# Split weights laid out in groups of four columns, with rings of their own for the two halves of the split

## The chip, the core and the metric

The kernel runs on one core of one Trainium2 chip. A core has a matrix engine (TensorE, PE in the profile, with its weight loads as PEld), a vector engine (VectorE, DVE), a scalar engine (ScalarE, ACT), GpSimd (POOL) and SyncE (SP), which here mainly issues DMA transfers. The on-chip memory SBUF has 128 partitions; TensorE reads its operands from SBUF and writes to PSUM, eight banks of 512 float32 per partition. The metric is the time of one execution on the device in microseconds; several runs are taken and their median is given.

## The reference

One layer of a decoder trunk in float32: 256 positions, model width 4096, 32 heads of 128. The convolution layer of the file is not reached (DEPTH is 1).

```python
h = x
h = h + attn_branch(rms_norm(h, norm_attn), w_in_attn, w_out_attn)
return rms_norm(h, final_norm)

def attn_branch(xn, w_in, w_out):
    q, k, v, g = split(xn @ w_in, 4)            # (256, 4096) @ (4096, 16384)
    o = stick_breaking_attention(q, k, v)       # per head, causal, in log space
    return (o * silu(g)) @ w_out                # (256, 4096) @ (4096, 4096)
```

The two projections are nearly all of the arithmetic. `stick_breaking_attention` needs, for each head, the scores z, a suffix sum over log(1 - sigmoid(z)), an exponential and a product with v.

## The kernel before

**Split operands.** [...] To keep float32 accuracy each operand is held as a high part (rounded by a copy into F32R) and a low part (the original minus the high part), and a product is three matmuls into one PSUM bank: high x high, high x low, low x high (`mm3`, lines 762 to 768). The stationary operand of such a matmul is a 128x128 block of activations, the moving operand 512 columns of weights.

**Units.** The weights' columns are cut into 20 units: 16 of the input projection (`units`, lines 268 to 271; each has the q, k, v and gate columns of two heads) and four of the output projection. A unit has 16 steps over the contraction, 256 rows each. At a step two weight tiles `raw` are loaded, [128, 2 blocks, 2 chunks of rows, 256 columns], from a ring of 7 (`load`, line 361). The first unit of each projection is "plain": 8 products a step. In the other units 10 of the 16 steps (`SEVEN`) get by with 7 products through sums of blocks, as in Strassen's method, and 6 take 8 products; in the last unit three more steps take 8. For the 7-product steps GpSimd issues a DMA that adds one chunk of rows to the other (`add_block`, line 380), and VectorE forms three more sums in place (`sums`, line 403).

**From raw weights to products.** `split` (line 442) walks the parts of the weights in the order of use. It takes a place in ring `w` (5 places, `PAIRS`: a high and a low tile [128, 2, 512] each) or, for parts of one chunk, in ring `s` (2 places), and starts `piece` (line 426): ScalarE copies `raw` to the high tile `wh` (a cast of 1024 or 512 elements per partition), VectorE subtracts (`minus`, line 264) and writes the low tile `wl`; then the raw tile may be given back (`low_done`). Both tiles hold their columns in one run: chunk c, then the two blocks of 256. `product` (line 1185) passes `wh[n][:, c, :]` and `wl[n][:, c, :]` to `mm3`. When a part's last product is through, `done` (line 1175) gives its place back.

**The order.** Nothing is decided on the chip. The class `Plan` (line 102) runs a small event simulation while the program is built: every piece of work has an engine, a cost, and a key (the time by which it is due, counted in products), and an engine takes the waiting work with the smallest key. `ring`, `take` and `give` are counters in that simulation which keep the number of live tiles of a tag under its number of buffers. The products themselves come in a fixed order (`products`, line 1197); TensorE's other work, that of the heads, goes between them.

**Beside the products.** When a unit's banks are full, `combine` (line 658) adds them into the tiles `one` and `two`; then the chain of its two heads (`heads`, `head`, `gated_with`, `gate`, lines 745 to 895) runs between the products of the next unit: transpose, scores, soft part on ScalarE and VectorE, suffix sum by a matmul with a triangle (`neg_tri`), exponential, product with v, gate. Its tiles have rings of one place each: `qkh`, `qkl`, `f`. The finished rows of two heads go out by DMA (`spill`) and come back as tile `p` for the output projection (`heads_of`, `blocks_of_heads`) through ring `gh`, which has three places. `gh` also serves the rows of x for the sums of squares (`x_stat`) and, at the end, the loads of x and of the final gain. The activations' stationary forms stay in SBUF all the time. During the output units the results `h` lie in a pool that takes the room of the attention's tiles (`make_room`, `new_h`), and the tail normalises and stores them.

Of the kernel before, what the change touches and what calls it, by code (L numbers as in the profile page):

```python
# [19 lines left out]
P = 128  # L20
S = 256
# [12 lines left out]

WARM, IDLE = 10, 640
# [8 lines left out]
PAIRS = 5  # L44
# [193 lines left out]
def kernel(  # L238
# [186 lines left out]

    def piece(n, c, there):

        p = parts[n]
        yield nc.until(*there)
        full = raw[p["tile"]][:, :, p["place"], :][:, :, c, :].rearrange("p i c n -> p c i n")  # L430
        h, l = (t[n][:, c, :].rearrange("p c (i n) -> p c i n", i=HG) for t in (wh, wl))
        size = (c.stop - c.start) * W
        key = first[n] - (AHEAD * 1e3 if p["seven"] and p["i"] < 2 else 0)
        yield act(lambda: nc.scalar.copy(h, full), size, key - 2.0 * 1e3)
        if n == 0:
            yield nc.until(("sh", c.start))
        yield dve(lambda: minus(l, full, h), size, key)
        for k in range(c.start, c.stop):
            nc.tell(("low", n, k))
        low_done(n)  # L440

    def split(size, tag, bufs):
        for n, p in enumerate(parts):
# [3 lines left out]
            yield nc.take(tag)  # L447
            t = p["tile"][1]
            yield nc.until(("raw", q, t))
            wh[n] = wp.tile([P, size, W], F32R, tag=tag + "h", name=f"wh{n}", bufs=bufs)  # L450
            wl[n] = wp.tile([P, size, W], F32R, tag=tag + "l", name=f"wl{n}", bufs=bufs)
# [8 lines left out]
    gcol = cp.tile([P, KC], F32, name="gcol")  # L460

# [47 lines left out]
    def blocks_of(i):  # L509

        key = place_of[0, i]
        tag = ("one", "two", "qkh", "qkl")[i % 4]
        yield nc.take(tag)
        y = ap.tile([P, KT, S], F32, tag=tag, name=f"xs{i}")
# [55 lines left out]
    for k in range(WARM):  # L570
        idle = wp.tile([P, IDLE], BF16, tag="gh", name=f"idle{k}", bufs=3)
        nc.vector.memset(idle, 0.0)
        nc.tensor.matmul(warm, idle[:, 0:P], idle[:, 0:W], start=True, stop=True)
# [11 lines left out]
    tri_f = ap.tile([P, P], F32, name="tri_f")  # L585
# [8 lines left out]
    def newton(r, v, name):  # L594

        e = cp.tile([P, 1], F32, name=f"{name}_e")
# [5 lines left out]
    ssq_x = cp.tile([P, NT, NQ], F32, name="ssq_x")  # L602
# [10 lines left out]
    def x_stat(i, t, q, w):  # L613
        xr = wp.tile([P, w], F32, tag="gh", name=f"xr{i}", bufs=3)
# [3 lines left out]
        yield nc.take("f")  # L618
        junk = ap.tile([P, w], F32, tag="f", name=f"junk{i}")
# [3 lines left out]
        nc.give("f", "gh")  # L623
        nc.tell(("stat", i))

    def x_factor():
        yield nc.until(*(("stat", i) for i in range(NT * NQ)))
        tot = cp.tile([P, NT], F32, name="ssq_xt")
# [6 lines left out]
        r = cp.tile([P, NT], F32, name="rin_r")  # L635
# [6 lines left out]
        rs["v"] = cp.tile([P, NT], F32, name="rin_v")  # L642
# [10 lines left out]
    def constants():  # L653
        yield nc.until(("used", 0, 1))
        yield dve(lambda: nc.vector.tensor_copy(neg_tri, tri_f), P)

# [88 lines left out]
    def gate(u):  # L745
# [3 lines left out]
        yield nc.take("qkl")  # L749
        l = ap.tile([P, NT, CW], F32, tag="qkl", name=f"gl{u}")  # L750
# [8 lines left out]
        nc.give("qkl")  # L759
# [17 lines left out]
    def head(u, i):  # L777
        yield nc.take("att", "qkh")
# [11 lines left out]
        qk = ap.tile([P, 2, S], F32, tag="qkh", name=f"qkT{u}_{i}")  # L790
# [11 lines left out]
        nc.give("qkh")  # L802
        yield nc.take("f")

        f = ap.tile([P, BW], F32, tag="f", name=f"f{u}_{i}")
# [17 lines left out]
        nc.give("f")  # L823
# [9 lines left out]
        nc.give("qkh", "qkl")  # L833
        yield nc.take("f")
        a = ap.tile([P, BW], F32, tag="f", name=f"a{u}_{i}")
# [20 lines left out]
        nc.give("f")  # L856
# [6 lines left out]
    def gated_with(u, i):  # L863
# [10 lines left out]
        if i == 0:  # L874
            yield nc.take("gh")
            st["o", u] = wp.tile([P, 4, P], F32, tag="gh", name=f"gated{u}", bufs=3)
# [20 lines left out]
    def heads_of(s, key, which=slice(0, 4)):  # L897

        yield nc.take("gh")
        y = wp.tile([P, 4, P], F32, tag="gh", name=f"p{s}", bufs=3)  # L900
# [39 lines left out]
    ssq_h = cp.tile([P, NT, NJ + 1], F32, name="ssq_h")  # L940
    mean_h = cp.tile([P, NT], F32, name="mean_h")
# [7 lines left out]
    def new_h(c):  # L949

        if c == NJ - 4:
# [4 lines left out]
        for t in range(NT):  # L956
            pool, tag, bufs = (ep, f"h{c}_{t}", 1)
            if c == NJ - 3 and t:
                pool, tag, bufs = wp, "gh", 3
# [13 lines left out]
    def load_out(c, t):  # L973
        pool, tag, bufs = (sp, "x" + "hl"[t] + str(LAST_STEPS[c - NJ + 4]), 1) if c >= NJ - 2 else (wp, "gh", 3)
# [6 lines left out]
    def load_gain(c):  # L981
        grow[c] = wp.tile([P, W], F32, tag="gh", name=f"grow{c}", bufs=3)
# [141 lines left out]
    def joined(t):  # L1124

        most[t] = cp.tile([P, 1], F32, name=f"most{t}")
# [4 lines left out]
    def finish(last, t, late):  # L1131
        v, r, f = (cp.tile([P, 1], F32, name=f"{n}{t}") for n in ("mean", "rout", "factor"))
# [42 lines left out]
    def done(n, k):  # L1175
# [4 lines left out]
        if count_down("part", n):  # L1180
            nc.give("w" if p["size"] == KT else "s")
# [3 lines left out]
    def product(n, k):  # L1185
# [6 lines left out]
            (wh[n][:, c, :], wl[n][:, c, :]),  # L1192
# [26 lines left out]
    together(split(KT, "w", PAIRS), split(1, "s", SINGLES), products(), x_stats(), x_factor(), constants())  # L1219
# [57 lines left out]
```

## Time and profile before

| | us |
|---|---|
| median of 3 runs (1739.35 to 1741.99) | 1740.06 |
| span of the profiled execution | 1738.8 |
| unit 0, from 8 to 94 us in the profile | 86.0 |
| one attention unit, 352.3 to 438.4 us | 86.1 |
| first output unit, 1385.9 to 1479 us | 93.1 |
| tail after the last matmul | 11.5 |

The profile is one execution of the program, taken by the hardware's profiler; the spans above are stretches of it. A row of the table by stretch gives the stretch, its length, then for each engine the time in which it was busy and how many instructions began, the granted TensorE clock as a share of the full one, the mean busy share of the DMA engines and the rate in GB/s. A row of a group of instructions gives line, engine, operation, output <- inputs, shapes and count, then the busy time in all, the mean length of one in ns, and the engine's idle time just before such instructions, with what ended it. Instructions of an engine overlap at their ends, so lengths are longer than the distance between two starts; for matmuls the ends are modelled, and only starts are used here. All instructions carry line 121, since one helper records them; they are told apart by their tiles: `acc` is a projection's PSUM bank, `sh`, `sl`, `oh`, `ol` are the stationary forms' parts, `z`, `tr`, `o` are the heads' banks.

### The profile page before, as it was taken

What the parts mean: (1) busy time and instruction counts of PE and PEld (TensorE: products, weight loads), DVE (VectorE), ACT (ScalarE), POOL (GpSimd) and SP (SyncE); (2) the same over time, 40 slices, a digit from 0 to 9 for tenths busy, and PEclk for the clock granted to TensorE, in tenths of its full rate; (3) what the DMA queues carried; (4) which work ended last, traced back from release to release, by engine and by line L of the source; (5) the groups of instructions that cost most, each with busy time, mean ns of one, the idle gap of its engine ahead of it and who ended that gap; (6) DMA issues with size and microseconds to landing.
All of it is one profiled execution on the core that took longest, in us unless ns stands there. A gap on an engine that the chain in (4) does not pass through costs nothing.

```text
span 1738.8 us, 24830 instructions
## 1 busy us (share of the span) xinstructions
PE 1722.9 (99%) x7735; PEld 1412.5 (81%) x7735; DVE 1643.5 (95%) x2106; ACT 1204.9 (69%) x1640; POOL 335.5 (19%) x407
## 2 busy tenths in 40 slices
PE   9999999999999999999999999999999999999997
PEld 6888888888888888888888888888888888878885
DVE  8889999999999999999999999999999987999997
ACT  7976767676767676767676767676767675666655
POOL 0022222222222221212222222222222112221220
PEclk9999999999999999999999999999999999999999
DMA  9967788878787878787878787878787878788895
GB/s 363 297 191 227 229 231 226 230 229 236 224 234 223 240 216 238 217 251 208 255 206 255 206 256 198 257 203 259 198 256 203 269 245 265 230 268 251 233 303 191
DMA packets 249380, 413.79 MB, mean 238 GB/s; under 512 B 28128, under 2 KB 73440, under 8 KB 249248
## 3 DMA queue, kind: packets, MB, share of 16 engines
q1 hardware_dynamic: 194544, 354.24, 60.6%
q0 software_dynamic: 54416, 57.70, 20.2%
q8 instruction: 60, 0.98, 0.2%
q14 instruction: 72, 0.59, 0.1%
q10 hardware_dynamic: 288, 0.28, 0.0%
HBM read 403.98 MB, written 8.13 MB: 237 GB/s over the span
## 4 chain that ended last, share of the span: by engine, by line
PE 78%; DVE 12%; issue 6%; ACT 2%; DMA 2%; SPq 0%; DVEq 0%; ACTq 0%
PE acc L121 74%; DVE wl L121 8%; DVE raw L121 3%; PE z L121 2%; PE o L121 1%; ACT wh L121 1%; DMA raw<-in_w_in_dram 1%; PE tr L121 1%; DVE gv_sb L121 1%; DVE h L121 0%; DMA raw<-in_w_out_dram 0%; DMA grow<-in_gain_out_dram 0%; DVE qk_sb L121 0%; SPq L121 0%; ACT sq L121 0%
## 5 line engine op out<-in xcount | busy, mean ns | idle before, releaser
L121 ACT CAST wh<-raw 128x1024 fp32r<-128x1024 f32 (+1 forms) x995 | 922.0, 971 | 406.1 <-issue 180.0
L121 DVE TENSOR_TENSOR wl<-raw,wh 128x1024 fp32r<-128x1024 f32 (+1 forms) x995 | 1068.8, 1123 | 58.4 <-ACT wh L121 56.6
L121 PE MATMUL acc<-wh,sh 128*128 128x512 f32 x1898 | 755.6, 398 | 0.0
L121 PE MATMUL acc<-wl,sh 128*128 128x512 f32 x1898 | 740.0, 390 | 0.8 <-DVE wl L121 0.8
L121 PE MATMUL acc<-wh,sl 128*128 128x512 f32 x1898 | 740.5, 390 | 0.0
L121 POOL DMA_DIRECT2D raw<-in_w_in_dram x300 | 262.9, 988 | 1078.9 <-DMA raw<-in_w_in_dram 427.4
L121 PEld LDWEIGHTS acc<-wh,sl 128*128 128x128 f32 x1898 | 356.3, 188 | 75.8 <-DVE sl L121 0.4
L121 PEld LDWEIGHTS acc<-wl,sh 128*128 128x128 f32 x1898 | 357.0, 188 | 73.8 <-DVE wl L121 2.8
L121 PEld LDWEIGHTS acc<-wh,sh 128*128 128x128 f32 x1898 | 356.8, 188 | 70.7 <-ACT wh L121 0.6
L121 DVE TENSOR_TENSOR raw<-raw,raw 128x512 f32<-128x512 f32 x354 | 243.4, 687 | 6.9 <-DMA raw<-in_w_out_dram 1.2
L121 PE MATMUL acc<-wl,oh 128*128 128x512 f32 x485 | 189.7, 391 | 2.0 <-DVE wl L121 1.8
L121 PE MATMUL acc<-wh,oh 128*128 128x512 f32 x485 | 190.0, 392 | 0.0
L121 PE MATMUL acc<-wh,ol 128*128 128x512 f32 x485 | 188.9, 389 | 0.0
L121 DVE TENSOR_TENSOR raw<-raw 128x512 f32<-128x512 f32 x177 | 121.0, 684 | 0.0
L121 PEld LDWEIGHTS acc<-wl,oh 128*128 128x128 f32 x485 | 91.1, 188 | 23.8 <-DVE wl L121 5.3
L121 PEld LDWEIGHTS acc<-wh,oh 128*128 128x128 f32 x485 | 91.0, 188 | 19.2 <-DVE gv_sb L121 0.5
L121 PEld LDWEIGHTS acc<-wh,ol 128*128 128x128 f32 x485 | 91.0, 188 | 18.8
L121 POOL DMA_DIRECT2D raw<-in_w_out_dram x54 | 47.1, 968 | 185.9 <-DVE wl L121 58.9
L121 ACT ACTIVATE f<-f 128x384 f32<-128x384 f32 x96 | 50.5, 526 | 3.0
L121 ACT COPY qkT<-tr 128x512 f32<-128x512 f32 x32 | 18.6, 581 | 24.1 <-PE tr L121 24.1
L121 ACT CAST oh<-p 128x512 fp32r<-128x512 f32 (+3 forms) x46 | 20.9, 467 | 18.8 <-DVE p L121 13.2
L121 DVE SCALAR_TENSOR_TENSOR gv_sb<-acc,rin_v,gv_sb 128x512 f32<-128x512 f32 x45 | 33.4, 741 | 0.0
(91 smaller groups left out, 750.3 us busy)
## 6 DMA issues: line engine op xcount, KB each, us to landing
raw<-in_w_in_dram SPq DMA_DIRECT2D x1024, 256.0 KB, 4.5
raw<-in_w_out_dram SPq DMA_DIRECT2D x256, 256.0 KB, 4.3
raw<-in_w_in_dram POOLq DMA_DIRECT2D x300, 128.0 KB, 4.7
p<-spill POOLq DMA_DIRECT2D x28, 256.0 KB, 4.2
raw<-in_w_out_dram POOLq DMA_DIRECT2D x54, 128.0 KB, 5.1
xr<-in_x_dram SPq DMA_DIRECT2D x16, 256.0 KB, 4.8
xres<-in_x_dram SPq DMA_DIRECT2D x16, 256.0 KB, 5.6
out_dram<-h SPq DMA_DIRECT2D x16, 256.0 KB, 2.8
```

The costliest lines, as they stand in the source:

```text
L121: return self.tc.keep_in_program_order(getattr(self.engine, name)(*args, **kw))
```

## The change

The diff does three things.

1. The high and low tiles of the weights are flat, [128, 1024], and are seen through `by_runs`: chunk c (2), block i (2) and groups of four columns are interleaved, so that a group of four neighbouring columns of one chunk and block lies in 16 bytes, and the next group of the same chunk and block starts sixteen elements further. The cast writes, the subtract reads and writes, and the matmul's moving operand reads with that pattern; `mm3` gives the PSUM side the same order of columns, so PSUM holds what it held. Parts of one chunk have both halves in one tile of ring `s`: the high part in the places of chunk 0, the low part in those of chunk 1.
2. Highs and lows have rings of their own: `w` with 7 highs, `wl` with 5 lows; the low place is taken after the cast has been given out.
3. Room is made for it. The heads' tiles `qkT`, `f`, `fh`, `fl`, `a` and the gate's `gl` go through ring `gh`, which has four places instead of three; two of the four tiles for x in unit 0 use ring `s`; the squares' scrap of `x_stat` goes to a PSUM bank; `tri_f` lies in a `gh` row until it is copied; small columns share one tile `scalars`; the sums of squares of x and of h share one tile; the results `h2` and `h3` lie in two high tiles and `h5` in two rows of `gh`.

```diff
+RUN = 4
-PAIRS = 5
+HIGHS = 7
+LOWS = 5
+ROWS = 4
...
-        ("raw", RAW_BUFS), ("w", PAIRS), ("s", SINGLES), ("gh", 3), ("one", 1), ("two", 1),
-        ("qkh", 1), ("qkl", 1), ("f", 1), ("att", 1), ("heads", 1),
+        ("raw", RAW_BUFS), ("w", HIGHS), ("wl", LOWS), ("s", SINGLES), ("gh", ROWS), ("one", 1), ("two", 1),
+        ("att", 1), ("heads", 1),
...
+    def by_runs(t):
+
+        return t.rearrange("p (h c i e) -> p c i h e", c=KT, i=HG, e=RUN)
+
     def piece(n, c, there):
...
-        full = raw[p["tile"]][:, :, p["place"], :][:, :, c, :].rearrange("p i c n -> p c i n")
-        h, l = (t[n][:, c, :].rearrange("p c (i n) -> p c i n", i=HG) for t in (wh, wl))
+        full = raw[p["tile"]][:, :, p["place"], :][:, :, c, :].rearrange("p i c (h e) -> p c i h e", e=RUN)
+        h = wh[n][:, c]
...
         yield act(lambda: nc.scalar.copy(h, full), size, key - 2.0 * 1e3)
+        if p["size"] == KT:
+            if c.start == 0:
+                yield nc.take("wl")
+                wl[n] = by_runs(wp.tile([P, KT * W], F32R, tag="wl", name=f"wl{n}", bufs=LOWS))
+                nc.tell(("lowslot", n))
+            else:
+                yield nc.until(("lowslot", n))
+        l = wl[n][:, c]
...
-            wh[n] = wp.tile([P, size, W], F32R, tag=tag + "h", name=f"wh{n}", bufs=bufs)
-            wl[n] = wp.tile([P, size, W], F32R, tag=tag + "l", name=f"wl{n}", bufs=bufs)
+            wh[n] = by_runs(wp.tile([P, KT * W], F32R, tag="wh" if size == KT else "s", name=f"wh{n}", bufs=bufs))
+            if size == 1:
+                wh[n], wl[n] = wh[n][:, 0:1], wh[n][:, 1:2]
...
+    scalars = cp.tile([P, 24], F32, name="scalars")
...
-        tag = ("one", "two", "qkh", "qkl")[i % 4]
+        tag = ("one", "two", "s", "s")[i % 4]
...
-        yield nc.take("f")
-        junk = ap.tile([P, w], F32, tag="f", name=f"junk{i}")
+        yield nc.take("att")
+        junk = att.tile([P, w], F32, tag="att", name=f"junk{i}")
...
     def mm3(out_, a, b, start, stop):
 
         (ah, al), (bh, bl) = a, b
+        if len(bh.shape) == 4:
+            out_ = out_.rearrange("p (i h e) -> p i h e", i=HG, e=RUN)
...
     def head(u, i):
-        yield nc.take("att", "qkh")
+        yield nc.take("att", "gh")
...
-        yield nc.take("f")
-
-        f = ap.tile([P, BW], F32, tag="f", name=f"f{u}_{i}")
+        yield nc.take("gh")
+
+        f = wp.tile([P, BW], F32, tag="gh", name=f"f{u}_{i}", bufs=ROWS)
...
-        yield nc.take("qkh", "qkl")
-        fh = ap.tile([P, BW], F32R, tag="qkh", name=f"fh{u}_{i}")
-        fl = ap.tile([P, BW], F32R, tag="qkl", name=f"fl{u}_{i}")
+        yield nc.take("gh", "gh")
+        fh, fl = (wp.tile([P, BW], F32R, tag="gh", name=f"f{k}{u}_{i}", bufs=ROWS) for k in "hl")
...
     def new_h(c):
 
+        if 2 <= c < NJ - 4:
+            pair = wp.tile([P, KT, W], F32, tag="wh", name=f"h{c}", bufs=HIGHS)
...
     def mixed_h(u, c):
         yield nc.until(("full", u, 1))
+        if c == 2:
+            yield nc.take("w", "w")
         if c == NJ - 4:
-            yield nc.take("raw", "gh")
+            yield nc.take("raw", "gh", "gh")
...
-            nc.give("w" if p["size"] == KT else "s")
+            nc.give(*(("w", "wl") if p["size"] == KT else ("s",)))
...
-            (wh[n][:, c, :], wl[n][:, c, :]),
+            (wh[n][:, c], wl[n][:, c]),
```

More of the change, by code (lines that the diff above doesn't have):

```diff
@@ L832, in head @@
         yield ten(scan, BW, BW, P, P)
-        nc.give("qkh", "qkl")
-        yield nc.take("f")
-        a = ap.tile([P, BW], F32, tag="f", name=f"a{u}_{i}")
+        nc.give("gh", "gh")
+        yield nc.take("gh")
+        a = wp.tile([P, BW], F32, tag="gh", name=f"a{u}_{i}", bufs=ROWS)
         def weights_of():
@@ L949, in new_h @@
     def new_h(c):
+        if 2 <= c < NJ - 4:
+            pair = wp.tile([P, KT, W], F32, tag="wh", name=f"h{c}", bufs=HIGHS)
+            for t in range(NT):
+                hs[c, t] = pair[:, t, :]
+            return
         if c == NJ - 4:
@@ L1131, in finish @@
     def finish(last, t, late):
-        v, r, f = (cp.tile([P, 1], F32, name=f"{n}{t}") for n in ("mean", "rout", "factor"))
+        v, r, f = (scalar_of_rows() for _ in range(3))
         second = ssq_h[:, t, NJ : NJ + 1]
```

68 lines of the change are left out of this document (40 added, 28 removed).

## The prediction

> **What bounds the kernel now.** I read the page's head first, then stretches of one projection unit each, then single matmuls.
>
> ```profile
> span 1738.8 us, 24830 instructions
> PE 1722.9 (99%) x7735; PEld 1412.5 (81%) x7735; DVE 1643.5 (95%) x2106; ACT 1204.9 (69%) x1640; POOL 335.5 (19%) x407
> PE 78%; DVE 12%; issue 6%; ACT 2%; DMA 2%; SPq 0%; DVEq 0%; ACTq 0%
> ```
>
> TensorE is busy for 99% of the span and holds 78% of the chain that ended last; VectorE stands just behind it with 95%. Busy shares alone do not say whether TensorE waits, so the next view is a table by stretch: unit 0, two attention units, the four output units, the tail.
>
> ```profile
> core 0: us, PE busy (x) PEld busy (x) DVE busy (x) ACT busy (x) POOL busy (x), PEclk, DMA share, GB/s
> 8.00:94.00 86.00, 85.23 (x373) 69.36 (x373) 74.45 (x132) 75.86 (x145) 3.85 (x5) 1.00 0.96 331
> 352.30:438.40 86.10, 86.10 (x392) 70.80 (x391) 82.95 (x102) 60.47 (x80) 18.40 (x23) 1.00 0.82 230
> 1299.80:1385.90 86.10, 85.92 (x391) 70.60 (x390) 82.84 (x102) 61.39 (x82) 18.06 (x22) 1.00 0.81 233
> 1385.90:1479.00 93.10, 93.06 (x423) 76.96 (x422) 77.76 (x133) 61.59 (x98) 15.48 (x26) 1.00 0.81 261
> 1479.00:1560.00 81.00, 79.88 (x350) 65.11 (x349) 78.25 (x97) 51.44 (x66) 15.63 (x18) 1.00 0.83 240
> 1560.00:1640.50 80.50, 79.57 (x348) 64.89 (x347) 80.15 (x96) 50.70 (x65) 18.56 (x22) 1.00 0.89 262
> 1640.50:1727.30 86.80, 86.77 (x381) 70.98 (x379) 82.34 (x115) 50.13 (x71) 11.01 (x13) 1.00 0.75 231
> 1727.30:1738.80 11.50, 0.00 (x0) 0.00 (x0) 4.21 (x12) 3.46 (x9) 0.00 (x0) 0.66 0.75 279
> ```
>
> In an attention unit (86.10 us) TensorE never stops, at the full granted clock (1.00). VectorE is busy 82.95 us of it, so 3.15 us remain there and 25.6 us on ScalarE. In the two middle output units VectorE already sets the pace: 80.15 of 80.50 us. So a unit can shorten in two ways only: a matmul takes less time, and VectorE then follows. What a matmul takes now comes from the chain in order of time (start, length, work) and from the timeline around one head:
>
> ```profile
> 307.05 0.81 PE o L121 x4
> 307.86 46.96 PE acc L121 x207
> 354.82 0.44 PE tr L121 x4
> ...
> 369.42 0.33 PE L121 MATMUL z<-fh,neg_tri 128*128 128x384 f32 x1
> 369.59 0.34 PE L121 MATMUL z<-fl,neg_tri 128*128 128x384 f32 x1
> 369.77 0.22 PE L121 MATMUL z<-fh,neg_tri 128*128 128x128 f32 x1
> ```
>
> 207 projection matmuls in 46.96 us are 226.9 ns each. Nothing but the stream of 512 columns fits in between: a 384-column matmul of the same kind starts its successor 0.17 us later (369.42 to 369.59), and 0.17/384 is 0.443 ns per column, as is 226.9/512. Time goes with the columns; there is no start cost to save. A mixed unit has 10 steps of 7 products and 6 of 8, 118 products of three matmuls, 354 x 0.2269 = 80.3 us; the remaining 5.8 us are its heads' own matmuls.
>
> **The change, part by part.** *Columns in groups of four.* The cast and the subtract write, and every projection matmul reads, runs of four elements (16 bytes) that lie sixteen elements apart. No instruction is added or removed. The rows it touches:
>
> ```profile
> L121 PE MATMUL acc<-wh,sh 128*128 128x512 f32 x1898 | 755.6, 398 | 0.0
> L121 PE MATMUL acc<-wh,oh 128*128 128x512 f32 x485 | 190.0, 392 | 0.0
> L121 ACT CAST wh<-raw 128x1024 fp32r<-128x1024 f32 x816 | 825.5, 1049 | 335.5 <-issue 138.8 <-PE acc L121 127.6 <-DVE raw L121 55.3
> ...
> L121 DVE TENSOR_TENSOR wl<-raw,wh 128x1024 fp32r<-128x1024 f32 x43 | 50.3, 1219 | 2.6 <-ACT wh L121 2.5
> L121 DVE TENSOR_TENSOR raw<-raw,raw 128x512 f32<-128x512 f32 x20 | 13.8, 688 | 0.3
> L121 DVE TENSOR_TENSOR wl<-raw,wh 128x512 fp32r<-128x512 f32 x10 | 6.8, 684 | 0.0
> ...
> 299.13 2.36 DVE L121 TENSOR_TENSOR wl<-raw,wh 128x1024 fp32r<-128x1024 f32 x2
> ```
>
> (The first three rows are counts of the whole run, the next three of the one unit 352.3 to 438.4, the last is from the timeline.) All 3 x (1898 + 485) = 7149 projection matmuls are concerned. No row shows a moving operand in short runs, so its price is bounded from both sides. Below, VectorE ends the gain: once a matmul is under (82.95 - 5.8)/354 = 217.9 ns, 9.0 ns less than now, the attention unit is VectorE's 82.95 us. Above, one lost column step for each group of four makes 226.9 x 5/4 = 283.6 ns. I take the lower end. The reason is that 0.443 ns per column is a rate, equal at 384 and 512 columns, so the feed of four-byte columns is what limits TensorE, and the order of addresses in that feed is the one thing of TensorE's work that the change alters. The rows give no sign, though; this is a choice and gets no more than its chance below. [...]
>
> For VectorE's and ScalarE's side I take nothing. The sums over raw (688 ns, two blocks of 256 with a hop) cost what the subtract in one run costs (684 ns); a hop after a long run is free, a hop after four elements no row shows. The subtracts of a unit are 50.3 + 6.8 = 57.1 us, so each per cent of stretch is 0.57 us on the engine that is to be the bound. The lower side could also be better: two subtracts in a row take 2.36 us, the second starting 1.14 us after the first, 0.08 less than its length, and the unit's 102 instructions packed in that way would fit in some 81 us. ScalarE's casts could take half as long again and still fit in its 25.6 us.
>
> *Separate rings.* Highs get seven places, lows keep five. Who waits today:
>
> ```profile
> ACT wh L121 <- PE acc L121: 150.0, 117, 3.5
> DVE wl L121 <- ACT wh L121: 56.6, 100, 1.7
> PE acc L121 <- DVE wl L121: 2.6, 5, 0.8
> ```
>
> ScalarE waits 150 us in all for a pair to come free from TensorE, VectorE 56.6 us for the cast, TensorE 2.6 us for the subtract. With TensorE as the bound, two more highs are worth at most those 2.6 us; with VectorE as the bound they let the casts run ahead and take away most of the 2.5 us per unit that VectorE idles before a subtract. That is what makes 82.95 us reachable and not 82.95 plus waits: no term of its own. The new wait for a low stands after the cast, with the same five lows as before, so nothing on ScalarE is queued behind it.
>
> *Heads' rows shared.* The heads' four private tiles go into the ring of four rows. By the chain above, head work ends at 307.86 and begins again at 354.82: 47 of 86.1 us are free, so the heads may run tens of us later before the next unit's results wait for their tiles: nothing. It bites where the last heads meet the loads of p, in the first output unit (1385.9 to 1479.0). I take 0.5 us there; its bounds are 0 and the heads' own 39 us (86.1 - 47) if they went wholly in series with the loads. The squares of x now go to a PSUM bank that no head uses in unit 0, the shared scalars serve a few small instructions at the end of unit 0 and in the tail: nothing, up to 1 us.
>
> **The sum**, against the profiled 1738.8 us: fifteen attention units, 15 x 3.15 = 47.2. Unit 0 has 384 matmuls, 384 x 9.0 ns = 3.5, but its DMA share is 0.96: I take 1.7. First output unit, 384 x 9.0 ns = 3.5 less 0.5: 3.0 (VectorE is at 77.76 of 93.10). Two middle output units: VectorE leaves 2.75 and 0.35, and most of that is waiting that it needs: 1.5 together. The last one: 363 x 9.0 ns = 3.3, VectorE leaves 4.46: 3.3. Tail of 11.5 us: 0. Together 56.7 us: 1682.1 us. The median of the runs is 1740.06, 1.3 us over the profiled time, so 1683.4 us.
>
> **The rivals.** *The groups cost TensorE nothing and bring nothing* (0.08). For it: runs as short as that might be one fetch like any other. TensorE then stays at 226.9 ns, everything else is hidden under it, and the time is 1738 to 1742 us. [...]
>
> *Each group costs TensorE a step* (0.14). If one step in seventeen is lost now and in future one for each group, a matmul takes 226.9 x 20/17 = 266.9 ns, and 7149 x 40 ns = 286 us: 2026 us; at 5/4 it is 2145 us. For it: the rate of 0.443 shows that something in this feed already has a limit; against it: nothing in the rows ties that limit to short runs. It decides from the first ns, since TensorE has no idle time.
>
> *VectorE's subtract stretches* (0.10). It reads one and writes one operand in groups. With TensorE unchanged it decides from 3.15/57.1 = 5.5% on; at 10% a unit is 2.6 us longer, twenty units some 50: 1790 us; at 25% 11.1 us a unit, 220 in all: 1960 us. Against it: every row of VectorE goes with the elements alone. [...]
>
> *The shared rows stall the first output unit* (0.04): forms of the heads come late and TensorE waits; with no gain elsewhere 5 to 20 us, 1745 to 1760 us. Against it: a loss that one unit can hold.
>
> **How the numbers follow.** My forecast has 0.64 with its own range of 1660 to 1720 us (VectorE packed to some 81 us per unit at the low end; a matmul that gains only a third of the 9 ns at the high end). Faster by over 0.2% (3.5 us, about what a measurement of this kernel can tell from no change) is that 0.64; within it 0.08; slower 0.14 + 0.10 + 0.04 = 0.28. To leave out no more than 2 in 10 the range must take in no change, the shared rows and the smaller stretches of VectorE, up to some 15%: 1660 to 1850 us. The step per group lies outside.
>
> **What would show it.** Right: in an attention stretch the chain gives 218 ns or less per projection matmul, VectorE is busy nearly without a gap, matmuls wait for wl, and the unit takes about 83 us. A matmul still at 227 ns is the first rival; 267 or more the second; a subtract of 128x1024 clearly over 1219 ns, the third; idle TensorE between 1386 and 1479 us of the old time, with casts of p late, the fourth. If the matmul is faster but the unit stays above 84 us, the forecast's step "VectorE can be packed" is wrong and not the one on the feed.

## The result, and the profile after

| | before | after |
|---|---|---|
| median of 9 runs each, us | 1740.23 (1739.06 to 1741.99) | 1736.38 (1734.59 to 1738.38) |
| ratio, 95% interval | | 0.9978 [0.9969, 0.9987] |
| span of the profiled execution, us | 1738.8 | 1734.4 |

The change saves 3.9 us; the forecast was 57. The time lies between the 1660 and 1850 us that the prediction gave in all, since these took in no change, and outside the 1660 to 1720 us of the forecast itself. (One of the six runs of *narrow*, further below, took 7647.81 us and is left out of its median.) The head of the profile page after, and its table by stretch (columns as before; all instructions now carry line 124):

```profile
span 1734.4 us, 25312 instructions
PE 1709.5 (99%) x7735; PEld 1413.1 (81%) x7735; DVE 1634.4 (94%) x2106; ACT 1209.9 (70%) x1640; POOL 334.7 (19%) x407
```

```profile
core 0: us, PE busy (x) PEld busy (x) DVE busy (x) ACT busy (x) POOL busy (x), PEclk, DMA share, GB/s
180.00:266.00 86.00, 84.93 (x389) 70.45 (x388) 82.64 (x103) 60.68 (x79) 17.23 (x21) 1.00 0.82 231
352.00:438.00 86.00, 85.62 (x392) 70.86 (x392) 81.86 (x101) 60.84 (x79) 18.25 (x22) 1.00 0.82 228
1386.00:1479.00 93.00, 93.00 (x428) 77.65 (x427) 76.42 (x132) 59.52 (x96) 14.90 (x25) 1.00 0.79 242
1637.00:1722.90 85.90, 85.55 (x378) 70.19 (x376) 81.72 (x115) 50.02 (x71) 10.99 (x13) 1.00 0.74 233
```

The work is what it was: 7735 matmuls, 2106 instructions on VectorE. The attention units are still about 86 us long, the clock is still 1.00, but TensorE, which was busy for 86.10 of 86.10 us, now stands for 1.1 and 0.4 us in the two shown. In the first output unit it does not stand at all.

For the length of units one instruction serves as a marker: ScalarE's `qk_sb<-gv_sb`, which runs once per attention unit. The view of that tile, before and after (count, shortest, median and longest in ns, then the first and the last start):

```profile
L121 ACT ACTIVATE qk_sb<-gv_sb,rin_v x15: 724/725/727, 178.8 to 1384.3; 128x512 f32<-128x512 f32 x15
```

```profile
L124 ACT ACTIVATE qk_sb<-gv_sb,scalars x15: 719/724/728, 180.2 to 1383.6; 128x512 f32<-128x512 f32 x15
```

Between the first and the last lie 14 units: 1205.5 us before (86.11 each), 1203.4 after (85.96 each). So of the 4.4 us between the two profiles, the start up to the first marker loses 1.4, the attention units gain 2.1 and the rest, output units and tail, 3.7 (1738.8 - 1384.3 = 354.5 against 350.8). This division of the span into three is used for every kernel below.

What one matmul takes is read from the chain in order of time (start, length, what), in the attention and the output units of the changed kernel:

```profile
1333.17 45.73 PE acc L124 x203
...
1455.04 82.93 PE acc L124 x368
```

45.73/203 and 82.93/368 are both 225.3 ns, where it was 226.9. The groups have saved 1.6 ns of a matmul, not 9.0. Times 7149 that is 11.4 us, and even of this only a third is seen. The row groups of one unit and of the whole run show that the other engines' instructions did not change in length:

```profile
L124 DVE TENSOR_TENSOR wl<-raw,wh 128x1024 fp32r<-128x1024 f32 x42 | 50.2, 1218 | 3.2 <-ACT wh L124 1.8 <-PE acc L124 1.3
L124 ACT CAST wh<-raw 128x1024 fp32r<-128x1024 f32 x816 | 826.0, 1046 | 294.5 <-DVE raw L124 183.0 <-PE acc L124 88.5 <-issue 11.9
```

The subtract takes 1218 ns (1219 before), the cast 1046 (1049). The table of waits (who waits for whom: us in all, times, longest) has new rows:

```profile
DVE wl L124 <- PE acc L124: 31.3, 46, 2.1
DVE wl L124 <- ACT wh L124: 30.9, 53, 0.9
PEld acc L124 <- DVE qk_sb L124: 13.6, 14, 1.5
PE acc L124 <- DVE qk_sb L124: 7.6, 14, 1.1
```

VectorE's waits for casts have fallen from 56.6 to 30.9 us, as the two more highs were meant to do (whether it is they is taken up under *pairs_again*), but 31.3 us of a new wait have come: VectorE stands with a subtract in hand until TensorE gives a low place back. And in 14 units TensorE now waits for `qk_sb`, a sum that `combine` does on VectorE when a unit's banks are full. No such row was there before. The timeline at one of these places (start, length, work, and in brackets the idle time before it and who ended it):

```profile
351.59 0.74 DVE L124 SCALAR_TENSOR_TENSOR qk_sb<-acc,scalars,qk_sb 128x512 f32<-128x512 f32 x1
352.25 0.68 DVE L124 TENSOR_TENSOR raw<-raw,raw 128x512 f32<-128x512 f32 x1
352.85 0.68 DVE L124 TENSOR_TENSOR wh<-raw,wh 128x512 fp32r<-128x512 f32 x1
353.45 0.68 DVE L124 TENSOR_TENSOR raw<-raw,raw 128x512 f32<-128x512 f32 x1
354.06 1.22 DVE L124 TENSOR_TENSOR wl<-raw,wh 128x1024 fp32r<-128x1024 f32 x1
355.19 0.74 DVE L124 SCALAR_TENSOR_TENSOR qk_sb<-acc,scalars,qk_sb 128x512 f32<-128x512 f32 x1
355.99 0.50 PE L124 MATMUL acc<-wh,sh 128*128 128x512 f32 x1 [0.38 <-DVE qk_sb L124]
```

VectorE works without a gap here, in its order; the second sum comes at 355.19 because other work stands before it in that order, and the bank that it frees comes too late for the matmul. VectorE's 3 us of idle time per unit did not keep it from being late.

### The profile page after: what moved, and what is told of

It reads as the page before. It is cut to its first block, busy times and chain, and to the rows that moved or that the text cites. A ratio compares the mean times of both kernels' runs of the same rounds, so it can differ in the third digit from the quotient of the medians.

```text
span 1734.4 us, 25312 instructions
## 1 busy us (share of the span) xinstructions
PE 1709.5 (99%) x7735; PEld 1413.1 (81%) x7735; DVE 1634.4 (94%) x2106; ACT 1209.9 (70%) x1640; POOL 334.7 (19%) x407
## 5 line engine op out<-in xcount | busy, mean ns | idle before, releaser
L124 DVE TENSOR_TENSOR wl<-raw,wh 128x1024 fp32r<-128x1024 f32 (+1 forms) x818 | 974.6, 1217 | 67.5 <-PE acc L124 31.3
L124 PE MATMUL acc<-wh,sh 128*128 128x512 f32 x2048 | 784.8, 395 | 8.1 <-DVE qk_sb L124 7.6
L124 PE MATMUL acc<-wh,sl 128*128 128x512 f32 x1898 | 732.8, 386 | 0.5 <-DVE sl L124 0.5
L124 PE MATMUL acc<-wl,sh 128*128 128x512 f32 x1748 | 675.7, 387 | 1.5 <-DVE wl L124 1.5
L124 PEld LDWEIGHTS acc<-wh,sh 128*128 128x128 f32 x2048 | 384.6, 188 | 92.4 <-DVE qk_sb L124 13.6
L124 PEld LDWEIGHTS acc<-wl,sh 128*128 128x128 f32 x1748 | 328.3, 188 | 63.9 <-DVE wl L124 4.4
L124 PE MATMUL acc<-wl,oh 128*128 128x512 f32 x458 | 177.3, 387 | 1.9 <-DVE wl L124 1.9
L124 DVE TENSOR_TENSOR wh<-raw,wh 128x512 fp32r<-128x512 f32 x177 | 120.8, 683 | 2.0 <-ACT wh L124 2.0
L124 PEld LDWEIGHTS acc<-wh,oh 128*128 128x128 f32 x512 | 96.0, 188 | 19.1
L124 PEld LDWEIGHTS acc<-wl,oh 128*128 128x128 f32 x458 | 85.8, 187 | 21.1 <-DVE wl L124 4.4
```

The source lines that it names most:

```text
L124: return self.tc.keep_in_program_order(getattr(self.engine, name)(*args, **kw))
```

## The experiments

First the change is taken apart, then a matmul's time, then a unit's; last comes the plan's price. The three columns of spans are the division above, in us, from each kernel's profiled execution; the last two columns are its runs. The kernel before, run beside them, had medians of 1739.9 us (layout_only to layout_paced), 1740.4 (sweeps_before to narrow_sums) and 1740.3 (the last two).

| kernel | first marker | one unit | rest | median of n, us | ratio, 95% interval |
|---|---|---|---|---|---|
| before | 178.8 | 86.11 | 354.5 | | |
| after | 180.2 | 85.96 | 350.8 | 1736.38 of 9 | 0.9978 [0.9969, 0.9987] |
| layout_only | 178.2 | 85.98 | 352.8 | 1736.71 of 11 | 0.9982 [0.9974, 0.9991] |
| rings_only | 179.5 | 86.33 | 352.9 | 1740.48 of 11 | 1.0004 [0.9995, 1.0013] |
| pairs_again | 177.8 | 85.63 | 360.0 | 1737.51 of 11 | 0.9985 [0.9976, 0.9994] |
| narrow | 176.2 | 85.99 | 352.2 | 1734.71 of 5 | 0.9972 [0.9960, 0.9984] |
| after_paced | 178.0 | 85.76 | 351.5 | 1732.68 of 5 | 0.9959 [0.9945, 0.9973] |
| layout_paced | 178.3 | 86.41 | 352.3 | 1743.12 of 11 | 1.0019 [1.0010, 1.0028] |
| sweeps_before | 177.8 | 86.39 | 355.9 | 1744.55 of 10 | 1.0025 [1.0015, 1.0034] |
| sweeps_rings | 180.4 | 86.34 | 355.5 | 1746.22 of 6 | 1.0038 [1.0025, 1.0051] |
| sweeps_paced | 181.5 | 86.50 | 369.1 | 1761.23 of 4 | 1.0118 [1.0103, 1.0133] |
| narrow_sums | 176.1 | 86.47 | 354.3 | 1741.64 of 10 | 1.0010 [1.0001, 1.0020] |
| narrow_low | 175.0 | 83.79 | 344.5 | 1695.53 of 4 | 0.9743 [0.9728, 0.9758] |
| narrow_rings | 178.7 | 85.51 | 349.0 | 1728.44 of 4 | 0.9934 [0.9917, 0.9950] |

Each division is of one execution. The runs of one kernel spread over 1.5 to 9 us, and the profiled execution of rings_only is the longest of its 11 (1742.71 us, 2.2 above their median), so tenths of a microsecond between two kernels' units are not certain.

### The change taken apart

*layout_only*: the kernel before with the groups of four alone (`by_runs`, flat tiles, the places of parts of one chunk); rings and heads' rows as before.

```diff
+    def by_runs(t):
+        return t.rearrange("p (h c i e) -> p c i h e", c=KT, i=HG, e=RUN)
```

> The kernel before with the groups of four alone, rings and heads' tiles as before. Theory A (the groups make each projection matmul shorter, from a start-to-start mean of 227.3 ns to 225.5 ns, and the new rings give part of it back): 7149 x 1.8 = 12.7 us less, 1727 to 1731 us, and no new wait of TensorE at the start of a unit. Theory B (the groups bring nothing, the rings the small gain): 1740 us, 227 ns per matmul.

*rings_only*: the changed kernel with its columns in one run again.

```diff
-        return t.rearrange("p (h c i e) -> p c i h e", c=KT, i=HG, e=RUN)
+        return t.rearrange("p (c i h e) -> p c i h e", c=KT, i=HG, e=RUN)
```

> The changed kernel with the weights' columns in one run per chunk and block again (chunk, block, column), everything else as changed. Theory A: the matmuls are back at 227.3 ns and the waits of the new rings stay, 1743 to 1750 us. Theory B: 1736 us.

The groups alone give 0.9982, all of the change's gain within the intervals; the rings and the shared rows alone give 1.0004, nothing that can be told from no change. The table says why the two do not add up to more: in the output units both gain (1.7 and 1.6 us, together 3.3, the change has 3.7), but in the attention units the rings lose 0.22 us a unit (86.33, in that longest execution) where the groups gain 0.13. Of the two expectations the one that gives the gain to the groups is nearer, but layout_only was to fall to 1731 us or less and rings_only to rise to 1743 or more; neither did. The same waits for `qk_sb` that the changed kernel has (7.6 us of TensorE's matmuls, 13.6 of its weight loads) are in the rings' kernel (3.9 and 10.2); with the old rings no matmul of a projection waits for it, and its weight loads do so only in layout_paced, 4.2 us in 14 places of at most 0.3.

One more thing goes with the rings, which the description of the change leaves out: a part of one chunk now takes its place in ring `s` after its raw tile has landed, not before (`split`). It is in rings_only, pairs_again and narrow_rings, and not in layout_only.

*pairs_again*: the changed kernel, but the low place is taken together with the high one, before the cast, instead of between cast and subtract.

```diff
-        if p["size"] == KT:
-            if c.start == 0:
-                yield nc.take("wl")
...
-                yield nc.take(tag)
+                yield nc.take(tag, "wl")
```

> The changed kernel, but the place for the low part is taken together with that for the high part, before the cast is given out, so that ScalarE and not VectorE waits for it. If VectorE's wait for a low place (31 us in 46 waits, new with the change) is what makes the sums at a unit's end late (TensorE waits 0.4 to 1.3 us per unit for them): those waits go, 1728 to 1732 us. If the late sums have another cause (the order of VectorE's work, the shared rows): 1735 to 1738 us.

Its waits:

```profile
ACT wh L124 <- PE acc L124: 204.3, 93, 3.7
DVE wl L124 <- ACT wh L124: 32.2, 73, 0.7
DVE wl L124 <- PE acc L124: 3.5, 5, 1.5
```

VectorE's wait for a low place falls from 31.3 to 3.5 us. ScalarE, which has room, now waits 204.3 us for TensorE instead of 133.1, though before the casts of single chunks and not of pairs (139.0 and 65.3 us; 44.6 and 88.5 in the changed kernel). The waits for `qk_sb` are gone, and the attention units take 85.63 us, 0.33 less than in the changed kernel. So the place of that wait, with the order that the plan wrote around it, is what made the sums late: a wait on VectorE stands before everything queued behind it, sums of banks among it. The time does not show it, because 9.2 us more go in the rest of the run, and about half of that at one place in the first output unit:

```profile
1447.82 0.75 PE L124 MATMUL acc<-wh,oh 128*128 128x512 f32 x1 [3.15 <-ACT oh L124]
1448.36 0.63 PE L124 MATMUL acc<-wl,oh 128*128 128x512 f32 x1
1448.79 0.63 PE L124 MATMUL acc<-wh,ol 128*128 128x512 f32 x1
```

A cast of activations (`oh`) is late, TensorE stands for 3.15 us, and for some 3 us after that its matmuls start every 430 ns. The granted clock from 1447.8 to 1451.8 us is 0.57 (0.91 over the 20 us from 1440 to 1460). The stall is a matter of the plan's order, which came out differently.

The run also bears on the two more highs. A high and a low are taken together and given back together here, so the plan never has more than five pairs out, as before the change. Still VectorE's waits for casts are 32.2 us, about what they are in the changed kernel (30.9), and in the three units from 344 to 602 us they are these, first in layout_only, then here:

```profile
DVE wl L122 <- ACT wh L122: 7.6, 15, 0.6
DVE wl L124 <- ACT wh L124: 5.2, 12, 0.6
```

Both kernels have the groups and at most five pairs; the first has units of 85.98 us, the second of 85.63. They differ by the heads' shared rows, the smaller changes that made room, the later place in ring `s`, and the plan's order. So it is not shown that two more highs shortened the waits for casts; the shared rows are a rival that no run tries by itself.

### What a matmul's time is made of

*micro_one*: a kernel that only multiplies, 24 cases of 30 matmuls in a row, operands at rest in SBUF; the reference's computation is left out. The cases change the moving operand's pattern or the stationary one's.

```diff
+        ("run", lambda k: mov[:, 0:512], seq),
+        ("onecolumn", lambda k: mov[:, 0:1].broadcast_to([P, 512]), seq),
+        ("oneweight", lambda k: mov[:, 0:512], lambda k: st[:, 0:1].broadcast_to([P, P])),
+        ("grpa", lambda k: groups(4, 16, 0), seq),
+        ("aftera", lambda k: after(0), seq),
...
+        ("half", lambda k: mov[:, 0:256], seq),
+        ("bf", lambda k: mb, lambda k: sbf[:, 128 * (k % 8) : 128 * (k % 8) + 128]),
```

> Leaves the whole computation out; 30 matmuls of 512 columns in a row per case, other engines idle, start-to-start times read. Theory C (the moving operand alone pays, one step per 64 bytes read): one run 227 ns, a moving operand of one column repeated 214 to 216 ns, a stationary operand of one column repeated still 227 ns, groups of four sixteen apart either 216 or 267 ns in all four positions alike. [...]

The chain in order of time; a case's length by 30 is its matmul, and the clock is 1.00 throughout:

```profile
29.24 6.80 PE run L178 x30
36.04 6.56 PE onecolumn L178 x30
42.60 6.88 PE oneweight L178 x30
49.48 6.87 PE grpa L178 x30
...
63.49 7.39 PE grpc L178 x30
...
78.01 6.67 PE aftera L178 x30
...
112.88 14.44 PE runtwo L178 x30
...
177.02 3.60 PE half L178 x30
180.62 3.30 PE quarter L178 x30
183.92 6.50 PE bf L178 x30
```

`run` is the kernel before: 226.7 ns. `half`, 256 columns, takes 120.0. The difference for 256 columns is 106.7 ns, 0.4167 ns each, and what is left over is 13.3 ns per matmul. Two sizes always give such a split; that the plan's price, 0.4167 x n + 13.4, has the same two numbers speaks for it. At 128 columns it does not hold: `quarter` takes 110.0 ns, not 66.7. Two-byte operands (`bf`) take 216.7 ns by the chain, 3.4 above 512 x 0.4167 = 213.3. What the 13 ns are is looked for in the cases that change one operand: one column repeated as moving operand takes 218.7 ns, so feeding the same word over and over takes away eight of them; one column repeated as stationary operand (`oneweight`, 229.3) takes away none; groups of four, sixteen apart, take 229.0 or 246.3 by where in the sixteen they begin (`grpa`, `grpc`); the changed kernel's own pattern 222.3 for one chunk and 227 for the other; and stationary blocks in steps of 2 to 16 words 233 to 235. Both operands' patterns matter, the stationary block's (226.7 against 233 to 235 ns) in a way that no run explains. The theory of the expectation does not hold: by it, groups of four were to take the same time at every place in the sixteen, where 229.0 and 246.3 ns came, and one column repeated as moving operand 214 to 216, where 218.7 came. The step per 64 bytes from which it starts was the author's supposition; no run shows it. What the 13 ns are stays open.

Runs of two words, sixteen apart (`runtwo`), take 481 ns, twice the time. So these groups of 8 bytes are far worse, and groups of four are not free by themselves: at `grpc` they cost 20 ns (246.3 against 226.7).

*micro_two*: the same with the kernel's own sequence, 28 products of three matmuls on seven highs and five lows, in 16 patterns; again the matmuls alone.

```diff
+        ("asbefore", plain, straight),
+        ("asafter", inter("h c i e"), straight),
...
+        ("ordsixteen", order(16, 4), placed(16, 4)),
...
+        ("longeight", order(4, 8), placed(4, 8)),
```

> Leaves the whole computation out; 28 products of three matmuls per case with the kernel's operand sizes (seven high and five low tiles, seven stationary blocks per step), other engines idle. With the columns in one run 227 ns; as in the change 222 to 227 ns. [...]

The tile view of four of them (the first of a product's three matmuls; shortest, median and longest in ns, first and last start):

```profile
L169 PE MATMUL asbefore<-wh,sh x28: 389/389/389, 30.9 to 49.3; 128*128 128x512 f32 x28
L169 PE MATMUL asafter<-wh,sh x28: 382/384/398, 50.0 to 68.2; 128*128 128x512 f32 x28
L169 PE MATMUL ordsixteen<-wh,sh x28: 434/438/448, 186.6 to 208.9; 128*128 128x512 f32 x28
L169 PE MATMUL longeight<-wh,sh x28: 380/381/399, 295.2 to 313.1; 128*128 128x512 f32 x28
```

Tenths of a microsecond are too coarse here; read to the hundredth from the timeline, from a case's first start to the last of its 84, a matmul takes 226.7, 225.6, 276.0 and 220.2 ns. The pattern of the change is worth 1.1 ns of the 13 with no other engine at work, somewhat less than the 1.6 in the kernel. Other orders of reading cost up to 50 ns, and one, four sweeps of eight words, wins 6.5. Both times of the expectation came: 226.7 ns where 227 was expected, 225.6 where 222 to 227 was.

*sweeps_before, sweeps_rings, sweeps_paced*: that order in the whole kernel; columns stay in one run, only the matmul reads (and PSUM is written) in four sweeps; in the kernel before, with the new rings, and with the plan's price of a matmul at 220 ns.

```diff
+        out_, bh, bl = (t.rearrange("p (h b e) -> p b h e", b=4, e=8) for t in (out_, bh, bl))
```

> The kernel before; only the projection matmuls read their 512 columns in another order, four sweeps over runs of eight columns that lie 32 apart, and write PSUM in that order (matmuls alone: 220.0 ns on the mean, against 226.7). If VectorE and its waits for casts set 86.0 us per attention unit, as with the shortened matmuls: 86.0 us per unit and 1733 to 1738 us, no better than 8.9 ns less per matmul. If TensorE were still the bound: 354 x 6.7 ns = 2.4 us less per unit, 1690 to 1700 us.

> The same reading order on the changed kernel's rings, with the columns stored in one run. It shows what pace VectorE keeps with seven highs, five lows and four shared rows. If the rings free VectorE from its waits (82 to 83 us busy per unit): 84 us per unit, 1700 to 1712 us. If they only move the waits (to low places and to the sums at a unit's end): 85.5 to 86 us, 1728 to 1736 us.

> The same with the planner's price of a 512-column matmul at 220 ns instead of 226.7. If the written order is what costs TensorE its waits: 5 to 15 us less than the same kernel with the old price; if VectorE's own chain is the bound: within 5 us of it.

All three are slower than before, by 0.25, 0.38 and 1.18%, and all three outside what was expected. Inside sweeps_before a matmul starts on average 228.4 ns after the one before it (mean of all distances up to 250 ns; 227.3 by the same count in the kernel before), not 220. The chain shows that this mean is a mixture:

```profile
184.45 11.90 PE acc L121 x54
...
220.77 47.78 PE acc L121 x207
...
270.97 12.46 PE acc L121 x54
```

In one unit 54 matmuls take 220.4 ns each, as they do alone; the 54 at the same place of the next unit take 230.7, and the 207 between them 230.8. The other work is alike in the two stretches of 54 (VectorE busy for 95% of both, DMA share 0.71 and 0.69), which speaks against a plain contest for the memory. What chooses between the two times is open; no run separates it.

### What holds a unit at 86 us

*narrow*: the kernel before with the second and third matmul of each product on 480 of the 512 columns (the low parts' products of the last 32 columns are left out). It makes TensorE faster without a pattern: by the same count of distances a matmul takes 220.4 ns on the mean instead of 227.3, 7 ns less where 8.9 were expected.

```diff
+        out_, bh, bl = out_[:, 0:NARROW], bh[:, 0:NARROW], bl[:, 0:NARROW]
         nc.tensor.matmul(out_, ah, bl, start=False, stop=False, **kw)
```

> The kernel before; the second and third matmul of each product take 480 of their 512 columns, the rest of the low parts' contribution is left out. That shortens a projection matmul by 32 x 2/3 x 0.4167 = 8.9 ns on the mean, the 9.0 ns of the forecast, and changes nothing else. If VectorE can be packed as the forecast had it: 83 us per attention unit and 1680 to 1690 us in all. If the written order and VectorE's queue hold it back (TensorE then waits for the sums at a unit's end and for the heads): 84 to 85.5 us per unit, 1700 to 1725 us.

A unit still takes 85.99 us, longer than either expectation, though TensorE alone needs only 83.8 (narrow_low, below). TensorE's waits for `wl` have risen from 2.6 to 17.3 us in the run. Two views of narrow, the table by stretch, and VectorE's waits in three units:

```profile
430.00:516.00 86.00, 84.81 (x392) 70.54 (x391) 82.94 (x102) 60.69 (x81) 18.04 (x21) 1.00 0.80 231
```

```profile
DVE wl L122 <- ACT wh L122: 7.6, 15, 0.6
DVE f L122 <- ACT f L122: 0.5, 3, 0.2
```

VectorE: 82.94 us busy, 2.5 us per unit in waits for casts of at most 0.6 us, 0.2 us for the heads; 85.6 in sum. It was as long as a unit already before the change, 0.1 us behind TensorE's 86.1.

*narrow_sums*: the same, with the sums of blocks planned 7 us ahead of their product instead of 3 (`SUMS_AHEAD`), to give VectorE other work while a cast runs.

```diff
-AHEAD, SUMS_AHEAD = 4.0, 3.0
+AHEAD, SUMS_AHEAD = 4.0, 7.0
```

> The kernel before with 480 of 512 columns in the second and third matmul of each product, and the planner's lead for the sums over raw raised from 3 to 7 us, so that a sum stands earlier in VectorE's order and its cast is done when VectorE comes to the subtract. If the waits of VectorE for these casts (2.5 us per unit) hold it at 86.0 us: those waits shrink and the unit falls to 83.5 to 85 us, 1690 to 1715 us. If the pace of 86.0 us has another cause: 86.0 us and 1735 us as before.

The units became longer (86.47), and the waits for casts rose from 51.2 to 58.8 us over the run. A miss: this knob does not fill the gaps.

*narrow_low*: narrow (on 240 of each 256 columns), and VectorE's subtract on 240 of 256 columns as well; the low parts of one column in sixteen are left out.

```diff
-        yield dve(lambda: minus(l, full, h), size, key)
+        yield dve(lambda: minus(l[:, :, :, 0:SHORT], full[:, :, :, 0:SHORT], h[:, :, :, 0:SHORT]), size, key)
```

> The kernel before, with the second and third matmul of each product on 2 x 240 of the 512 columns, as in the narrow run, and VectorE's subtract on 240 of the 256 columns of each block (1024 elements become 960). TensorE's floor per attention unit falls to about 83 us as in narrow; VectorE's work falls by 57.1 x 1/16 = 3.6 us, some 3.2 us counted by starts. If VectorE's own work plus its waits set the 86.0 us in narrow: units of 83 to 83.5 us, 1685 to 1697 us in all. If something else holds the unit (ScalarE's casts, the order of the plan, the loads): units stay at 85.5 to 86.0 us and 1728 to 1736 us. Left out: the low parts of one column in sixteen.

```profile
430.00:516.00 86.00, 86.00 (x404) 73.12 (x403) 82.30 (x105) 61.92 (x81) 18.00 (x21) 1.00 0.83 233
```

The unit falls to 83.79 us and TensorE has no idle time again; the run takes 1695.53 us. Against narrow only VectorE's subtract was shortened (the matmuls have as many columns, in two pieces), so VectorE's own work and waits held the unit at 86 us. This fits layout_only too: its matmuls alone would let a unit end at 86.11 - 354 x 0.0016 = 85.54 us, but it takes 85.98, what narrow takes with the same rings.

*narrow_rings*: the changed kernel with columns in one run and with narrow's short matmuls. This is the premise of the forecast (TensorE well under VectorE) with the change's rings.

```diff
+        bh, bl = (t.rearrange("p i h e -> p (i h e)") for t in (bh, bl))
+        out_, bh, bl = out_[:, 0:NARROW], bh[:, 0:NARROW], bl[:, 0:NARROW]
```

> The changed kernel with its columns in one run again (as in rings_only) and the second and third matmul of each product on 480 of the 512 columns. TensorE's floor per attention unit is about 83 us, so VectorE's pace with seven highs and five lows shows. If the new rings let VectorE be packed, as the prediction had it: units of 83 to 84 us, 1685 to 1705 us. If VectorE's place in line is what it was (86.0 us in narrow with the old rings): units of 85.6 to 86.2 us, 1728 to 1738 us. If the wait for a low, standing in VectorE's line, costs pace: units over 86.3 us, 1740 us or more. Left out: the low parts' products of the last 32 columns of each bank.

```profile
DVE wl L125 <- ACT wh L125: 5.4, 9, 0.6
DVE wl L125 <- PE acc L125: 3.2, 6, 0.7
```

In the same three units VectorE waits 5.4 us for casts instead of 7.6, and 3.2 us for low places instead of none: 2.9 us a unit against 2.5 and 0.2. A unit takes 85.51 us, 0.48 less than with the old rings, and the run 1728.44 us. The rings, with the shared rows and the order that come with them, do raise VectorE's pace, by some half a microsecond a unit; they do not pack it. In the changed kernel VectorE's 85.51 and TensorE's 85.54 us are then all but equal; that each wait of one for the other is therefore seen in the time is argued from these two numbers.

### The plan's price

*after_paced, layout_paced*: the changed kernel, and layout_only, with the plan's price of a matmul lowered by 1.2 ns, most of the 1.6 that the groups save.

```diff
 def tensor_ns(n):
-    return 0.4167 * n + 13.4 if n > 128 else 109.0
+    return 0.4167 * n + 12.2 if n > 128 else 109.0
```

> The changed kernel with the same price of 225.5 ns in the planner. If the order written for a slower TensorE costs the waits at the units' starts (0.4 to 1.3 us each): 1728 to 1733 us; else 1735 to 1738 us.

> The groups alone, with the planner's price of a 512-column matmul lowered from 226.7 to 225.5 ns, so that it writes the order for the pace that the groups bring. If the gain is lost because TensorE comes to the heads' matmuls and to the unit's end sooner than the order foresees: 1728 to 1733 us. If VectorE simply has no room: 1735 to 1738 us as without it.

With the change it is the fastest kernel of the study that computes all that the reference asks: 1732.68 us, 0.9959 [0.9945, 0.9973], 3.7 us below the change itself. TensorE's waits for `qk_sb` fall:

```profile
PEld acc L124 <- DVE qk_sb L124: 10.2, 14, 1.2
PE acc L124 <- DVE qk_sb L124: 4.2, 14, 0.8
```

from 13.6 and 7.6 us, and a unit from 85.96 to 85.76 us. In layout_only the same price makes the kernel 6.4 us slower (units of 86.41). So the price helps only with the new rings; why the old rings lose by it no run shows.

## Why the prediction was wrong

**"Time goes with the columns; there is no start cost to save."** This is the first step that failed. The two durations from which it came, 0.17 us at 384 columns and 226.9 ns at 512, cannot tell a rate from a rate with a start cost: 0.4167 x 384 + 13.4 is 173 ns, which the timeline shows as 0.17 too. The 256-column matmul tells them apart, at 120.0 ns (0.443 x 256 would be 113). By these two sizes some 213 of a matmul's 226.7 ns go with the columns at 0.4167 ns each, and no 512-column case of either micro kernel took less (216.7 the lowest); by that reckoning the groups could work only on the other 13. The kernel said so itself: the plan's price, line 99 of the kernel before, is that very formula, and the prediction did not use it.

**"I take the lower end"**, a matmul of 217.9 ns or less. The sign was right, the size was not: 1.6 ns, not 9.0. The 9.0 were no estimate of the matmul but what VectorE's busy time would let through, and the choice rested on the rate that the first step had misread; that it came out on the faster side at all was luck. The matmuls alone show that patterns of groups lie between 220 and 276 ns, with no rule that was found.

**"VectorE can be packed"**, to its busy time of 82.95 us. This step failed by itself, and would have spoilt the forecast even with the first one right. The prediction took VectorE's 3.15 idle us per unit as room that two more highs would open. They were 2.5 us of waits for casts and gaps between; VectorE stood 0.1 us behind TensorE (narrow, 85.99 us). With TensorE well below VectorE and the change's rings, a unit is 85.51 us and the run 1728.44: some 12 us gained, not 57. That two more highs would take away "most of the 2.5 us" held for less than a third in steady units, 0.7 us (7.6 to 5.4 us in three units), and the low ring put 1.1 us in its place; and since pairs_again has 5.2 us there with no more than five pairs out, even that third is not shown to be the highs' work. In the terms of the sum, the attention units' 47.2 us came out as 2.1, the output units' 7.8 as 3.7, and unit 0's 1.7 as a loss of 1.4 up to the first marker.

**"Nothing on ScalarE is queued behind it"**, the wait for a low. True, and beside the point: the wait is on VectorE, and the sums of a full bank are queued there. The prediction left out the queue in which the moved step then stands. With the wait moved back, and another order (pairs_again), a unit takes 85.63 us, so that nearly all of 1.6 ns x 354 = 0.57 us per unit is seen, where the change shows 0.15.

**Groups cost VectorE and ScalarE nothing.** Right: 1218 and 1046 ns against 1219 and 1049. The rival of a stretched subtract is out.

**Heads' rows shared: nothing, half a microsecond in the first output unit.** Right as far as it was tested: TensorE is busy in 93.00 of 93.00 us there. The shared rows were not tried by themselves, only with the rings; under pairs_again they may even be what helps.

**The rivals.** *Nothing at all, 1738 to 1742 us* came nearest: its time is missed by 1.6 us, but its premise, a matmul that stays at 226.9 ns, is not what happened; the gain was small and partly given back. *A step per group* did not happen: nothing near 267 ns came of this pattern, 225.3 in the kernel; the lost step in seventeen from which its 266.9 were worked out was a supposition that no run shows. (In micro_one runs of four took up to 246 ns, runs of two 481.) The prediction's last sentence, that with faster matmuls and units above 84 us the packing is at fault, is half of the answer: the matmuls were hardly faster either.

## What to carry to other kernels

Idle time of the second-busiest engine is not free room until its waits have been taken apart: shorten the busiest engine's work (here by leaving columns out) and see whether the time follows, before a layout is built for it. When a step takes a buffer later than before, ask in which engine's line it now waits, and what stands behind it there. Two sizes that lie close together cannot tell a rate from a start cost; use a far one, and read the prices that the kernel's own planner already has.

## What the runs showed of the chip

- Matmuls on F32R operands with a new stationary block each take 226.7 ns at 512 columns and 120.0 at 256, as 0.4167 ns per column and some 13 ns more per matmul would give; 128 columns take 110.0. Two-byte operands take 216.7 at 512 (micro_one).
- The time of 512 columns moves with the pattern of both operands: 218.7 with one moving column repeated, 229 to 246 for groups of four by their place in sixteen words, up to 276 for other orders, 481 for runs of two words, and 233 to 235 with the stationary block's columns 2 to 16 words apart (micro_one; the 276 micro_two).
- A pattern's time with matmuls alone need not hold in the kernel: four sweeps of eight took 220.2 ns alone, and in the kernel 220.4 in one stretch and 230.7 at the same place of the next unit (micro_two, sweeps_before).
- After a stall of 3.15 us, TensorE's matmuls started every 430 ns for some 3 us, at a granted clock of 0.57 over those 4 us (pairs_again).
